# Second mixer: attention heads and state space written as steps beside the units, in a kept order, four units split ahead

## The chip, the cores and the metric

The kernel runs on one core of a Trainium2 chip. The metric is device time in microseconds (us) per execution, and a time is the median of several runs. The engines are TensorE (PE in the profile, with PEld for its weight loads), VectorE (DVE), ScalarE (ACT), GpSimd (POOL) and SyncE (SP), which issues the weight loads from memory.

## What is computed

A network on one sequence of 256 positions with 1024 channels, in float32: a first block of two layers and then a second block of two layers. The change touches only the mixer of the second block, which runs twice. Cut to it, the reference is:

```python
h = rms_norm_2(x, mix_norm[i])
proj = h @ w_in[i]
z, xbc, dt_raw, q, k, v = jnp.split(proj, splits, axis=-1)
xbc = jax.nn.silu(causal_depthwise_conv(xbc, conv_w[i], conv_b[i]))
y_ssd = ssd_mixer(xbc, dt_raw, z, dt_bias[i], a_log[i], d_skip[i], ssd_norm[i])
q = rms_norm_2(q.reshape(b, s, ATT_HEADS, ATT_HEAD_DIM), q_norm[i])   # 16 heads of 64
k = rms_norm_2(k.reshape(b, s, ATT_HEADS, ATT_HEAD_DIM), k_norm[i])
y_att = dilated_attention(q, k, v.reshape(b, s, ATT_HEADS, ATT_HEAD_DIM)).reshape(b, s, ATT_WIDTH)
x = x + jnp.concatenate([y_ssd, y_att], axis=-1) @ w_out[i]
```

`ssd_mixer` takes `dt = softplus(dt_raw + dt_bias)`, decays each of 16 heads by `exp` of a running sum of `dt * a` in two chunks of 128 positions, adds `x * d_skip`, gates by `silu(z)` and normalises in four groups. `dilated_attention` sums three strided windows, which the kernel does as one softmax with a mask and a table of multiplicities.

## The kernel before

The program has eleven stages in a row: ada0 and the even mixer, peer0, the odd mixer, peer1, and then ffn1_0, mix_0, ffn2_0, ffn1_1, mix_1, ffn2_1. mix_0 and mix_1 are two calls of `second_mixer` with their own weights, and only they and the order of their weights change.

Weights come as tiles of 1 MB, which SP loads (L154) into `w_raw`. One tile holds two *units* of 128x1024. Each float32 product is made of three products in a shorter format: a unit is copied by ACT into its high part `w_hi` (L171), and its low part `w_lo` is a subtraction (L162) on DVE or on POOL, as the letters of `E.pattern` say ("V" or "P", in turn). `w_hi` and `w_lo` have three buffers in the earlier stages; once L1590 has been passed, in ffn1_0, there are four of each and three of `w_raw`. A unit of a projection is then 24 matmuls of 128x256 (`mm3`, L199 to L201; L229 to L231 where the result has rows of positions).

A mixer uses 48 units for the input projection and 16 for the output. Its order in the text is: 16 units of q and k, each multiplied by the rms (L1384), squared (L338) and summed per head (L339); behind the second pair the parts of the normalised input `xn` (L1391) and the section that makes `dt` and its running sum `acum`; `rstd` of the sums; 8 units of v (`gemm_rows`); 8 blocks of two attention heads, each with two spreads of the norm (`spread2`, L357 and L358), scores (L1442 to L1445), softmax, transposes and the product with v (`attend`); 16 units of the convolution (first 8 `bc`, then 8 `xs`), each with one ACT and three DVE instructions (L1469, L1472) and a silu (L1460, L1461); the products of `bc` after its eighth, transposes of `xs` after each fourth; 8 units of `z` with a silu; then the state space, 8 blocks of two heads: a spread, three Relu (L1511), an Exp (L1513), two multiplications that give the decayed products `m` (L1515), two matmuls (L1518, L1519), the gate (L1521, L1522), a square (L1524) and its group sum (L1525); 8 units of the output projection for the attention's half (`accum` of blocks 8 to 15); `rstd` of the group sums; the normalised `y` in parts (L1537, L464, L465) and 8 units for the other half; and the residual (L423).

What runs when is not this order. A scheduler that knows only what depends on what and which buffers are free places the instructions of each engine, and puts heads, convolutions, state space and units between each other; only places in `in_order` keep the order of the text, and the second mixer has none.

Of the kernel before, what the change touches and what calls it, by code (L numbers as in the profile page):

```python
# [34 lines left out]
ADA = [b for c in range(8) for b in (8 + c, c)] + list(range(16, 96))  # L35

# [29 lines left out]
class Net:  # L66
# [108 lines left out]
    def units(self, ap):  # L175

        for k in range(ap.shape[0]):
# [4 lines left out]
    def prefetch(self, ap):  # L182

        u = self.units(ap)
# [244 lines left out]
    def attend(self, W, ps, mult, vrow, pv, o, between=None):  # L429
# [23 lines left out]
        pt = self.tp.tile([128, 512], F32, name="tp")  # L453
# [890 lines left out]
def second_mixer(E, i):  # L1344
# [3 lines left out]
    with ExitStack() as ctx:  # L1348
# [3 lines left out]
        yl = S.tile([128, 16, T], F32R, name="yl")  # L1352
        at = ctx.enter_context(tc.tile_pool(name="at", bufs=2, space=PSUM, side=E.side, reuse_waits="tile"))
        pvp = ctx.enter_context(tc.tile_pool(name="pv", bufs=1, space=PSUM, side=E.side, reuse_waits="tile"))
        E.tp = tp = ctx.enter_context(tc.tile_pool(name="tp", bufs=1, space=PSUM, side=E.side, reuse_waits="tile"))
# [4 lines left out]
        units = E.stage_units(io[f"mix_{i}_in"])  # L1360
# [6 lines left out]
        nc.gpsimd.dma_start(maskb, io["dilate_mask"])  # L1367
        identb = S.tile([128, 128], BF, name="identb")
        nc.vector.tensor_copy(identb, E.ident)
# [4 lines left out]
        for u in range(0, 16, 2):  # L1374
            pss = [mm.tile([128, T], F32, name="mm"),
                   pvp.tile([128, T], F32, name="pv") if u == 2 else mm.tile([128, T], F32, name="mm")]
            ws = [next(units) for _ in range(2)]
            if u == 0:
                E.gemms(pss, ws)
                rms = E.rms(tp.tile([128, T], F32, name="tp"))  # L1380
            for k in range(2):
                if u:
                    E.gemm(pss[k], ws[k])
                nc.vector.tensor_tensor(qk[:, u + k], pss[k], rms, op=OP.mult)  # L1384
                E.head_stat(W, stat[:, u // 8], qk[:, u + k], (u + k) % 8, 8, T, start=u + k == 0,
                            stop=(u + k) % 8 == 7)
            if u == 2:

                for c in range(NB):
                    t = E.nrm.tile([128, T], F32, name="sq", bufs=4)  # L1390
                    nc.vector.scalar_tensor_tensor(t, E.x[:, c], scale(c), rms, op0=OP.mult, op1=OP.mult)  # L1391
                    E.parts(xn[0][:, c], xn[1][:, c], t)

                dw = W.tile([128, 128], F32, name="dw", bufs=1)
                nc.scalar.dma_start(dw, io[f"mix_{i}_dt"])
                ps = at.tile([128, T], F32, name="at")
                E.gemm(ps[:16], E.split(dw, 128), 16, xn)
                dt, acum = (S.tile([16, T], F32, name=n) for n in ("dt", "acum"))
                e, t1, l, one = (t[:, k] for t in (S.tile([16, 2, T], F32, name=n) for n in ("r_hi", "r_lo"))
                                 for k in range(2))  # L1400
                db = E.s("dt_bias", i, p=16)
                nc.vector.memset(one, 1.0)
                nc.scalar.activation(t1, ps[:16], AF.Abs, bias=db)
                nc.scalar.activation(e, t1, AF.Exp, scale=-1.0)

                zero, ea = (S.tile([16, 1], F32, name=n) for n in ("zero", "ea"))
                nc.vector.tensor_scalar(zero, e[:, :1], 0.0, None, op0=OP.mult)
                nc.scalar.activation(ea, E.s("a_log", i, p=16), AF.Exp, bias=zero)
                nc.vector.tensor_scalar(dt, ps[:16], db, 0.0, op0=OP.add, op1=OP.max)
                log1p(E, l, e, t1)  # L1410
                nc.vector.tensor_tensor(dt, dt, l, op=OP.add)
                nc.vector.tensor_scalar(e, dt, ea, -1.0, op0=OP.mult, op1=OP.mult)
                for c in range(2):
                    sl = slice(c * 128, c * 128 + 128)
                    nc.vector.tensor_tensor_scan(acum[:, sl], one[:, sl], e[:, sl], 0.0, op0=OP.mult, op1=OP.add)
                rel = S.tile([16, 128], F32, name="rel")
                nc.vector.tensor_scalar(rel, acum[:, :128], acum[:, 127:128], None, op0=OP.subtract)
                ps = at.tile([128, 5, 16], F32, name="at")
                for k, src in enumerate((acum[:, :128], rel, acum[:, 128:], dt[:, :128], dt[:, 128:])):
# [335 lines left out]
```

## Time and profile before

| | us |
|---|---|
| median of 3 runs (3502.95 to 3520.05) | 3516.53 |
| the profiled execution | 3519.85 |
| its span in the profile | 3518.1 |
| mix_0, from 2308.9 to 2622.3 | 313.4 |
| mix_1, from 3006.9 to 3325.3 | 318.4 |

Over the whole span PE is busy for 97%, DVE for 67%, ACT for 53% and POOL for 27%. A mixer is read in three pieces that the trace marks well: the *start*, from the rms matmul (L323) to the first v matmul (L229); the *middle*, from there to the first Relu of the state space (L1511); and the *gated part*, from there to the residual (L423). In a row of the windows, the number behind an engine is its busy time and x its instructions; PEclk is the granted TensorE clock, 1.00 for 2.4 GHz and 0.50 for 1.2 GHz.

### The profile page before, as it was taken

What the parts mean: (1) busy time and instruction counts of PE and PEld (TensorE: products, weight loads), DVE (VectorE), ACT (ScalarE), POOL (GpSimd) and SP (SyncE); (2) the same over time, 40 slices, a digit from 0 to 9 for tenths busy, and PEclk for the clock granted to TensorE, in tenths of its full rate; (3) what the DMA queues carried; (4) which work ended last, traced back from release to release, by engine and by line L of the source; (5) the groups of instructions that cost most, each with busy time, mean ns of one, the idle gap of its engine ahead of it and who ended that gap; (6) DMA issues with size and microseconds to landing.
All of it is one profiled execution on the core that took longest, in us unless ns stands there. A gap on an engine that the chain in (4) does not pass through costs nothing.

```text
span 3518.1 us, 64405 instructions
## 1 busy us (share of the span) xinstructions
PE 3402.0 (97%) x26071; PEld 3169.4 (90%) x26071; DVE 2362.8 (67%) x4428; ACT 1881.7 (53%) x3561; POOL 937.1 (27%) x451
## 2 busy tenths in 40 slices
PE   5889999999999999999999999999999999999999
PEld 5679999999997579999999999977889999877899
DVE  5776878888885566878877776566654454665544
ACT  3444677644445445677644445446554444565443
POOL 0034000144443135000044444441142332302422
PEclk8989999999999899999999999999999999998899
DMA  6435444477774125444355555532335545423254
GB/s 251 179 114 185 167 150 148 144 263 269 271 261 153 37 73 180 168 145 147 142 191 186 186 191 193 180 137 97 120 110 189 182 180 182 148 94 110 98 190 144
DMA packets 85851, 576.64 MB, mean 164 GB/s; under 512 B 9855, under 2 KB 11248, under 8 KB 20016
## 3 DMA queue, kind: packets, MB, share of 16 engines
q1 hardware_dynamic: 82448, 567.35, 44.9%
q8 instruction: 204, 3.34, 0.4%
q0 software_dynamic: 1520, 3.30, 0.3%
q10 hardware_dynamic: 1584, 1.88, 0.2%
q14 instruction: 95, 0.78, 0.1%
HBM read 571.54 MB, written 1.34 MB: 163 GB/s over the span
## 4 chain that ended last, share of the span: by engine, by line
PE 85%; DVE 7%; ACT 3%; issue 1%; DMA 1%; POOL 0%; DVEq 0%; ACTq 0%; POOLq 0%
PE acc L200 15%; PE acc L201 14%; PE acc L199 14%; PE mm L199 9%; PE mm L201 9%; PE mm L200 9%; PE g L976 2%; PE g L978 2%; DVE w_lo L162 1%; ACT w_hi L171 1%; DMA w_raw<-peer_v 1%; PE at L357 1%; DVE wl L465 1%; PE stat L339 1%; PE pv L1518 1%
## 5 line engine op out<-in xcount | busy, mean ns | idle before, releaser
L171 ACT ACTIVATE w_hi<-w_raw 128x1024 fp32r<-128x1024 f32 x980 | 1037.4, 1059 | 1005.0 <-PE acc L200 416.3
L162 POOL TENSOR_TENSOR w_lo<-w_raw,w_hi 128x1024 fp32r<-128x1024 f32 x357 | 866.7, 2429 | 2351.5 <-ACT w_hi L171 1594.7
L162 DVE TENSOR_TENSOR w_lo<-w_raw,w_hi 128x1024 fp32r<-128x1024 f32 x623 | 765.7, 1229 | 339.1 <-ACT w_hi L171 322.3
L199 PE MATMUL mm<-xh,w_hi 128*128 128x256 f32 (+1 forms) x2568 | 734.9, 287 | 16.5 <-ACT xh L332 8.7
L200 PE MATMUL mm<-xl,w_hi 128*128 128x256 f32 (+1 forms) x2568 | 731.0, 285 | 3.1 <-DVE xl L333 1.6
L201 PE MATMUL mm<-xh,w_lo 128*128 128x256 f32 (+1 forms) x2568 | 730.5, 285 | 1.2 <-DVE w_lo L162 1.2
L200 PE MATMUL acc<-wl,w_hi 128*128 128x256 f32 x2048 | 574.5, 281 | 7.0 <-DVE wl L465 6.9
L199 PE MATMUL acc<-wh,w_hi 128*128 128x256 f32 x2048 | 573.8, 280 | 3.3 <-ACT wh L464 3.3
L201 PE MATMUL acc<-wh,w_lo 128*128 128x256 f32 x2048 | 573.6, 280 | 0.0
L199 PEld LDWEIGHTS mm<-xh,w_hi 128*128 128x128 f32 (+1 forms) x2568 | 488.7, 191 | 32.1 <-issue 18.5
L200 PEld LDWEIGHTS mm<-xl,w_hi 128*128 128x128 f32 (+1 forms) x2568 | 488.1, 190 | 11.1 <-DVE xl L286 4.2
L201 PEld LDWEIGHTS mm<-xh,w_lo 128*128 128x128 f32 (+1 forms) x2568 | 489.8, 191 | 5.0 <-DVE w_lo L162 2.4
L199 PE MATMUL acc<-xh,w_hi 128*128 128x256 f32 (+1 forms) x1536 | 449.1, 292 | 16.5 <-ACT xh L530 10.4
L200 PE MATMUL acc<-xl,w_hi 128*128 128x256 f32 (+1 forms) x1536 | 443.3, 289 | 15.6 <-DVE xl L532 15.1
L465 DVE TENSOR_TENSOR wl<-ring,wh 128x256 fp32r<-128x256 f32 x256 | 361.4, 1414 | 128.0 <-ACT wh L464 128.0
L201 PE MATMUL acc<-xh,w_lo 128*128 128x256 f32 (+1 forms) x1536 | 442.2, 288 | 0.1
L200 PEld LDWEIGHTS acc<-wl,w_hi 128*128 128x128 f32 x2048 | 385.5, 188 | 8.7 <-DVE wl L465 8.6
L199 PEld LDWEIGHTS acc<-wh,w_hi 128*128 128x128 f32 x2048 | 385.5, 188 | 3.7 <-ACT wh L464 3.7
L201 PEld LDWEIGHTS acc<-wh,w_lo 128*128 128x128 f32 x2048 | 385.5, 188 | 0.0
L199 PEld LDWEIGHTS acc<-xh,w_hi 128*128 128x128 f32 x1536 | 300.4, 196 | 18.9 <-ACT xh L530 11.3
L200 PEld LDWEIGHTS acc<-xl,w_hi 128*128 128x128 f32 x1536 | 298.3, 194 | 19.5 <-DVE xl L532 16.9
L201 PEld LDWEIGHTS acc<-xh,w_lo 128*128 128x128 f32 x1536 | 299.4, 195 | 1.7 <-issue 0.9
(452 smaller groups left out, 5961.7 us busy)
## 6 DMA issues: line engine op xcount, KB each, us to landing
w_raw<-ffn SPq DMA_DIRECT2D x132, 1024.0 KB, 4.8
w_raw<-peer_u SPq DMA_DIRECT2D x128, 1024.0 KB, 4.8
w_raw<-peer_v SPq DMA_DIRECT2D x128, 1024.0 KB, 4.8
w_raw<-mix_in SPq DMA_DIRECT2D x48, 1024.0 KB, 4.7
ring<-ada SPq DMA_DIRECT2D x56, 512.0 KB, 5.7
ada<-ada SPq DMA_DIRECT2D x20, 1024.0 KB, 4.8
w_raw<-mix_out SPq DMA_DIRECT2D x16, 1024.0 KB, 4.8
w_raw<-even_in SPq DMA_DIRECT2D x12, 1024.0 KB, 6.2
```

The costliest lines, as they stand in the source:

```text
L162: ins = e.tensor_tensor(out, a, hi, op=OP.subtract)
L171: self.nc.scalar.activation(hi[:, :n], src, AF.Copy)
L199: mm(ps, wh, xh, start=start, stop=False, skip_group_check=True)
L200: mm(ps, wh, xl, start=False, stop=False, skip_group_check=True)
L201: mm(ps, wl, xh, start=False, stop=stop, skip_group_check=True)
L339: self.nc.tensor.matmul(ps, self.esel[:, 30 - 2 * b:30 - 2 * b + 2 * nb], sq[:, :w], start=b == 0 if start is None else start, stop=b == n ...
L357: self.nc.tensor.matmul(ps, sel, hi, start=True, stop=False)
L465: return self.nc.vector.tensor_tensor(yl, src, yh.bitcast(F32), op=OP.subtract).ins
L976: nc.tensor.matmul(ps[:, t], oi[:, :, t], o1[:, :, t], start=t == 0, stop=False, skip_group_check=True)
L978: nc.tensor.matmul(ps[:, t], oi[:, :, t], o2[:, :, t], start=False, stop=t == TB - 1, skip_group_check=True)
L1518: mm_(pv[o:o + 64], xr[:, 0, hs], m[:, :256], start=True, stop=False, skip_group_check=True)
```

## The change

The units of the input projection come in another order (`MIX_IN`, of tiles of two units): two tiles of convolution, then one of z. The whole mixer keeps the order of its text on PE, DVE, ACT and SP (`in_order`). A `Flow` splits units up to four ahead, with pattern "V", so that every subtraction of the mixer is DVE's; 33 of 65 were POOL's in mix_0. The start multiplies four units before it squares any, makes the parts of `xn` one per unit, and leaves the `dt` section to `steps()`, whose pieces follow the units of the convolution one by one. Attention is made of ticks: tick t makes the scores of head t-1, the transposes of head t-2, the two spreads of block t/2 if t is even, and the product with v of head t-3. A unit of v in the second half and a unit of z has one tick before it, a unit of convolution 0.4. Transposes take the banks `tp` and `st` in turn. The second half of a silu (`pending`) waits for the next tick or unit, products and transposes of `xs` (`later`) for one unit each. In the gated part a block is: the gate of the block before, one output unit (blocks 0 to 5), the group sums, the decay of the next two heads, and the two matmuls of each of its own heads. Units 14 and 15 of the output follow the last block, with `rstd` between them, and `finish` of block b+2 stands behind unit b.

Cut to its core, the diff is (removed lines stand in the functions above):

```diff
+MIX_IN = list(range(12)) + [12, 13, 20, 14, 15, 21, 16, 17, 22, 18, 19, 23]
...
-        units = E.stage_units(io[f"mix_{i}_in"])
+        flow = Flow(E, chain(E.stage_units(io[f"mix_{i}_in"]), E.units(io[f"mix_{i}_out"])), 2)
+        order.enter_context(E.in_order(*(e.engine for e in (nc.tensor, nc.vector, nc.scalar, nc.sync))))
...
+        first = [bank(), bank(), bank(), pvp.tile([128, T], F32, name="pv")]
+        flow.split()
+        E.gemms(first[:2], [next(flow), next(flow)])
+        flow.split(3)
+        E.gemm(first[2], next(flow))
+        rms = E.rms(tp.tile([128, T], F32, name="tp"))
+        flow.split()
+        E.gemm(first[3], next(flow))
+        flow.split()
+        for u in range(4):
+            scaled(u, first[u])
+        for u in range(4):
+            squared(u)
+        nc.vector.tensor_copy(identb, E.ident)
+        for u in range(4, 16):
+            ps = bank()
+            E.gemm(ps, next(flow))
+            stats()
+            scaled(u, ps)
...
+            flow.split()
+            squared(u)
+            if c < NB:
+                E.parts(xn[0][:, c], xn[1][:, c], t)
...
+        def steps():
...
+            E.gemm(ps[:16], dws, 16, xn)
...
+            nc.scalar.activation(l, t1, AF.Ln)
+            yield
...
+        def tick(t):
+            def between():
+                if t > 1:
+                    next(heads[t - 2], None)
+                while pending:
+                    pending.pop()()
+                if t < 16 and t % 2 == 0:
+                    spread(t // 2)
+            if 1 <= t < 17:
+                head(t - 1, between)
+            else:
+                between() if t < 18 else None
+            if t >= 3:
+                next(heads[t - 3], None)
+                if (t - 3) % 2:
+                    blk = (t - 3) // 2
+                    E.parts(yh[:, 8 + blk], yl[:, 8 + blk], pvs[-1])
...
+        for p in MIX_IN[12:]:
+            for u in (2 * p - 24, 2 * p - 23):
+                attention(1 if u >= 16 else 0.4)
+                ps = bank()
+                E.gemm(ps, next(flow), x=xn)
+                if later:
+                    later.popleft()()
...
+                next(pieces, None)
+        attention(19)
...
+        def out(k):
+            E.accum(acc, next(flow), yh[:, k], yl[:, k], k == 8, k == 7)
+            flow.split()
+
+        decay(0)
+        decay(1)
         for blk in range(8):
+            while pending:
+                pending.pop()()
+            if blk < 6:
+                out(8 + blk)
+            gated()
+            if blk < 7:
+                decay(2 * blk + 2)
+                decay(2 * blk + 3)
+            states(blk)
+        pending.pop()()
+        out(14)
+        gated()
+        r = E.rows(S, "s", E.rstd(E.nrm, stat[:4, 0], [4, T], 256), lambda t: t[:4, 0], [16, 2, T])
+        out(15)
...
+        finish(0)
+        finish(1)
+        for blk in range(8):
+            out(blk)
+            if blk < 6:
+                finish(blk + 2)
```

What it does to the rows of an engine is shown at three places of mix_0. Lines above 36 move down by 4 and those of the mixer by more, so L162 is L166 after, and L1384 is L1391. The first place is the start, on DVE; `rs_v` is the rms, `dw` the weights of `dt`, and `tp`, `mm` and `pv` are banks of accumulators. Before:

```order
L162 TENSOR_TENSOR w_lo<-dw,w_hi 128x128
L252 TENSOR_SCALAR rs_v_27247<-tp 128x256
L253 SCALAR_TENSOR_TENSOR rs_v_27247<-rs_v_27247,rs_r_27248 128x256
L254 TENSOR_TENSOR rs_v_27247<-rs_v_27247,rs_r_27248 128x256
L255 SCALAR_TENSOR_TENSOR rs_v_27247<-rs_v_27247,rs_r_27248 128x256
L1384 TENSOR_TENSOR qk<-mm,rs_v_27247 128x256 x3
L162 TENSOR_TENSOR w_lo<-w_raw,w_hi 128x1024
L1384 TENSOR_TENSOR qk<-pv,rs_v_27247 128x256
```

And after:

```order
L166 TENSOR_TENSOR w_lo<-w_raw,w_hi 128x1024 x3
L256 TENSOR_SCALAR rs_v_27299<-tp 128x256
L257 SCALAR_TENSOR_TENSOR rs_v_27299<-rs_v_27299,rs_r_27300 128x256
L258 TENSOR_TENSOR rs_v_27299<-rs_v_27299,rs_r_27300 128x256
L259 SCALAR_TENSOR_TENSOR rs_v_27299<-rs_v_27299,rs_r_27300 128x256
L166 TENSOR_TENSOR w_lo<-w_raw,w_hi 128x1024 x2
L1391 TENSOR_TENSOR qk<-mm,rs_v_27299 128x256 x3
L1391 TENSOR_TENSOR qk<-pv,rs_v_27299 128x256
```

The subtraction of `dw` has left the place ahead of the rms, and two subtractions of units stand between the rms and the first multiplication by it.

The second place is one pair of attention heads in the middle, on PE. Before, the scheduler's order (r_hi and r_lo are the spreads' operands, identb and maskb the mask of the scores, pts the transposed weights of a head):

```order
L455 MATMUL tp<-cst,p 128x128
L199 MATMUL mm<-yh,w_hi 128x256
L455 MATMUL tp<-cst,p 128x128 x2
L200 MATMUL mm<-yl,w_hi 128x256
L201 MATMUL mm<-yh,w_lo 128x256
L199 MATMUL mm<-yh,w_hi 128x256
L357 MATMUL at<-r_hi,bsel 128x256
L358 MATMUL at<-r_lo,bsel 128x256
L200 MATMUL mm<-yl,w_hi 128x256
L460 MATMUL pv<-pts,v 64x256
L461 MATMUL pv<-pts,v 64x128
L201 MATMUL mm<-yh,w_lo 128x256
```

After, one tick between two units:

```order
L1504 MATMUL at<-maskb,identb 128x384
L1505 MATMUL at<-qk 128x128
L1507 MATMUL at<-qk 128x256
L459 MATMUL stat<-cst,p 128x128 x3
L361 MATMUL at<-r_hi,bsel 128x256
L362 MATMUL at<-r_lo,bsel 128x256
L361 MATMUL at<-r_hi,bsel 128x256
L362 MATMUL at<-r_lo,bsel 128x256
L464 MATMUL pv<-pts,v 64x256
L465 MATMUL pv<-pts,v 64x128
L203 MATMUL mm<-yh,w_hi 128x256
```

The matmuls of the heads, which stood singly among those of a unit, stand in one piece between two units.

The third place is the gated part, on ACT: decay of the heads (Relu, Exp), the gate's square, and the copies of the units. Before:

```order
L1511 ACTIVATE m<-at,col 128x128 x4
L1513 ACTIVATE m<-m 128x384
L1511 ACTIVATE m<-at,col 128x128
L1524 ACTIVATE sq<-v 128x256
L1511 ACTIVATE m<-at,col 128x128
L171 ACTIVATE w_hi<-w_raw 128x1024
L1513 ACTIVATE m<-m 128x384
```

After, blocks 5 to 7 (p and pts are the decayed products of an even and of an odd head):

```order
L1659 ACTIVATE sq<-z 128x256
L175 ACTIVATE w_hi<-w_raw 128x1024
L1639 ACTIVATE p<-at,col 128x128 x3
L1641 ACTIVATE p<-p 128x384
L1639 ACTIVATE pts<-at,col 128x128 x3
L1641 ACTIVATE pts<-pts 128x384
L1659 ACTIVATE sq<-z 128x256
L1639 ACTIVATE p<-at,col 128x128 x3
L1641 ACTIVATE p<-p 128x384
L1639 ACTIVATE pts<-at,col 128x128 x3
L1641 ACTIVATE pts<-pts 128x384
L1659 ACTIVATE sq<-z 128x256 x2
```

Every block has the same five pieces in the same order, and in blocks 6 and 7 no unit's copy stands among them.

## Rows read from the trace of the kernel before

**Rows 1.** Stretches: window, length, busy (x) of PE PEld DVE ACT POOL, PEclk, DMA, GB/s

```profile
2200.00:2240.00 40.00, 40.00 (x338) 40.00 (x337) 21.84 (x26) 18.35 (x25) 16.79 (x7) 1.00 0.53 185
2312.90:2379.10 66.20, 58.74 (x393) 47.41 (x392) 37.03 (x58) 28.01 (x46) 22.99 (x10) 0.92 0.36 129
3010.80:3066.80 56.00, 53.99 (x393) 44.74 (x392) 32.78 (x61) 28.05 (x46) 13.02 (x7) 1.00 0.43 152
2379.10:2529.20 150.10, 148.53 (x937) 120.97 (x935) 96.81 (x241) 90.21 (x178) 24.89 (x12) 1.00 0.31 111
3066.80:3216.90 150.10, 149.04 (x940) 121.38 (x938) 98.19 (x242) 90.25 (x178) 21.88 (x11) 1.00 0.31 111
2529.20:2616.60 87.40, 84.69 (x484) 64.62 (x485) 37.22 (x73) 44.11 (x99) 33.27 (x14) 0.88 0.25 89
3216.90:3319.60 102.70, 98.79 (x482) 72.09 (x482) 37.19 (x73) 44.22 (x99) 33.15 (x14) 0.73 0.21 75
3231.90:3272.90 41.00, 41.00 (x122) 23.27 (x121) 10.55 (x29) 15.88 (x42) 4.69 (x2) 0.50 0.07 26
2545.00:2585.00 40.00, 40.00 (x228) 26.80 (x228) 18.53 (x43) 24.45 (x59) 11.87 (x5) 1.00 0.15 54
```

**Rows 2.** Timeline, start of mix_0: start, length, engine, line, [idle before <-releaser]

```profile
2312.95 5.15 DVE L162 TENSOR_TENSOR w_lo<-dw,w_hi 128x128 fp32r<-128x128 f32 x1 [0.21 <-PE mm L200]
2320.84 2.74 PE L339 MATMUL stat<-sq,cst 128*16 128x256 f32 x6 [3.60 <-ACT sq L338]
```

**Rows 3.** Timeline of PE in the even mixer: one head's matmuls between two units

```profile
126.31 0.34 PE L626 MATMUL at<-maskb,identb 128*128 128x384 bf16 x1
128.70 0.38 PE L357 MATMUL at<-r_hi,bsel 8*128 8x256 f32 x1
129.37 0.39 PE L199 MATMUL mm<-xh,w_hi 128*128 128x256 f32 x1
```

**Rows 4.** Groups by line, middle of mix_0: count | busy us, mean ns | idle before

```profile
L171 ACT ACTIVATE w_hi<-w_raw 128x1024 fp32r<-128x1024 f32 x33 | 34.9, 1058 | 31.8 <-PE mm L200 21.9 <-PE mm L231 6.8 <-issue 3.0
L162 POOL TENSOR_TENSOR w_lo<-w_raw,w_hi 128x1024 fp32r<-128x1024 f32 x12 | 29.4, 2452 | 130.1 <-ACT w_hi L171 130.1
L162 DVE TENSOR_TENSOR w_lo<-w_raw,w_hi 128x1024 fp32r<-128x1024 f32 x22 | 26.9, 1222 | 18.1 <-ACT w_hi L171 18.0
L1469 ACT ACTIVATE cv<-mm,sm 128x256 f32<-128x256 f32 x16 | 8.9, 556 | 0.1
L1472 DVE SCALAR_TENSOR_TENSOR cv<-mm,sm,cv 128x254 f32<-128x254 f32 x16 | 7.7, 481 | 0.5
L437 DVE TENSOR_REDUCE nm<-at 128x1 f32<-128x128 f32 x16 | 4.7, 291 | 8.2 <-PE at L1445 7.9
L1490 PE MATMUL tp<-cst,xs 128*128 128x128 f32 x16 | 3.6, 297 | 1.0 <-DVE xs L1461 1.0
L1478 PE MATMUL tp<-bc 128*128 128x256 f32 x8 | 2.7, 424 | 0.0
L1479 PE MATMUL tp<-bc 128*128 128x128 f32 x8 | 1.5, 274 | 0.0
```

**Rows 5.** Timeline of ACT in the middle of mix_0: Exp of one head's scores

```profile
2417.26 0.72 ACT L442 ACTIVATE p<-at,nm 128x128 f32<-128x128 f32 x2
```

**Rows 6.** Timeline, gated part of mix_0: one block's pieces on ACT, DVE and PE

```profile
2554.10 0.88 ACT L1511 ACTIVATE m<-at,col 128x128 f32<-128x128 f32 x3 [0.75 <-PE pv L1519]
2555.64 0.51 ACT L1513 ACTIVATE m<-m 128x384 f32<-128x384 f32 x1
...
2557.68 0.59 PE L1525 MATMUL tp<-sq,cst 128*4 128x256 f32 x2
2557.80 0.75 DVE L1515 SCALAR_TENSOR_TENSOR m<-m,col,cbm 128x256 f32<-128x256 f32 x2 [0.87 <-ACT m L1513]
...
2558.21 0.65 PE L1518 MATMUL pv<-m,bc 128*64 128x256 f32 x2
...
2559.00 0.38 PE L357 MATMUL at<-acum_hi,identr 16*128 16x256 f32 x1
```

More of the change, by code (lines that the diff above doesn't have):

```diff
@@ L173, in split, with units @@
         return hi, lo
-    def units(self, ap):
-        for k in range(ap.shape[0]):
+    def units(self, ap, order=None):
+        for k in order or range(ap.shape[0]):
             t = self.load(ap[k])
@@ L1367, in second_mixer @@
         nc.gpsimd.dma_start(maskb, io["dilate_mask"])
+        dw = W.tile([128, 128], F32, name="dw", bufs=1)
+        nc.scalar.dma_start(dw, io[f"mix_{i}_dt"])
         identb = S.tile([128, 128], BF, name="identb")
-        nc.vector.tensor_copy(identb, E.ident)
         v = S.tile([128, 2, D], F32, name="v")
         xn = yh[:, :NB], yl[:, :NB]
-        stat = st.tile([16, 2, T], F32, name="stat")
[L1374 to L1380, printed above, removed]
-            for k in range(2):
[L1382 to L1419, printed above, removed]
-                    nc.tensor.transpose(ps[:, k], src, E.ident[:16, :16])
-                col = S.tile([128, 5, 16], F32, name="col")
-                nc.vector.tensor_copy(col, ps)
-                acum = E.rows(S, "acum", acum)
@@ new lines, in second_mixer, with turned, spread @@
+        heads, pvs, turns = {}, [], [0]
+        def turned():
+            turns[0] += 1
+            return (tp, st)[turns[0] % 2].tile([128, 512], F32, name=("tp", "stat")[turns[0] % 2])
+        def spread(blk):
+            ps = at.tile([128, 2, T], F32, name="at")
+            for k in range(2):
+                E.spread2(ps[:, k], r, k, blk)
+            for k in range(2):
+                u = 8 * k + blk
+                nc.vector.scalar_tensor_tensor(qk[:, u], qk[:, u], E.s("k_norm2" if k else "q_norm2", i), ps[:, k],
+                                               op0=OP.mult, op1=OP.mult)
@@ new lines, in sums, with head @@
+        def sums(h):
+            if h % 2 == 0:
+                pvs.append(pvp.tile([128, T], F32, name="pv"))
+            return pvs[-1]
+        def head(h, between):
+            blk, o = h // 2, h % 2 * 64
+            ps = at.tile([128, 384], F32, name="at")
+            mm_(ps, identb, maskb, start=True, stop=False, skip_group_check=True)
+            mm_(ps[:, 0:128], qk[o:o + 64, blk, 0:128], qk[o:o + 64, 8 + blk, 0:128], start=False, stop=False,
+                skip_group_check=True)
+            mm_(ps[:, 128:384], qk[o:o + 64, blk, 128:256], qk[o:o + 64, 8 + blk], start=False, stop=True,
+                skip_group_check=True)
+            heads[h] = E.attend(W, ps, mult, [v[:, tt, h * 64:h * 64 + 64] for tt in range(2)], lambda: sums(h), o,
+                                between, turned)
+            next(heads[h])
@@ new lines, in second_mixer, with decay @@
+        attention(19)
+        while later:
+            later.popleft()()
+        for _ in pieces:
+            pass
+        ctx2.close()
+        acc = E.accs(ctx.enter_context(tc.tile_pool(name="acc", bufs=1, space=PSUM, side=E.other(), reuse_waits="tile")))
+        stat = tp.tile([16, 2, T], F32, name="tp")
+        ms = {}
+        def decay(h):
+            ps = at.tile([128, T], F32, name="at")
+            E.spread(ps, E.identr[:, h:h + 1].to_broadcast([16, 128]), *acums)
+            m = ms[h] = W.tile([128, 384], F32, name=("p", "pts")[h % 2])
+            for k, sl in enumerate((slice(0, 128), slice(128, 256), slice(128, 256))):
+                nc.scalar.activation(m[:, k * 128:k * 128 + 128], ps[:, sl], AF.Relu, bias=col[:, k, h:h + 1],
+                                     scale=-1.0)
+            nc.scalar.activation(m, m, AF.Exp, scale=-1.0)
+            for k, sl in enumerate((slice(0, 256), slice(256, 384))):
+                nc.vector.scalar_tensor_tensor(m[:, sl], m[:, sl], col[:, 3 + k, h:h + 1], cbm[:, h // 4, sl],
@@ L1526, in second_mixer @@
-        E.pattern = "P"
-        units = E.units(io[f"mix_{i}_out"])
-        for k in range(8, 16):
-            E.accum(acc, next(units), yh[:, k], yl[:, k], k == 8, False)
-        r = E.rows(S, "r", E.rstd(E.nrm, stat[:4, 0], [4, T], 256), lambda t: t[:4, 0], [16, 2, T])
-        for blk in range(8):
+                m, hs = ms.pop(h), slice(h * 64, h * 64 + 64)
+                mm_(pv[o:o + 64], xr[0][:, 0, hs], m[:, :256], start=True, stop=False, skip_group_check=True)
+                mm_(pv[o:o + 64, 128:], xr[0][:, 1, hs], m[:, 256:], start=False, stop=True, skip_group_check=True)
@@ L1541, in second_mixer @@
+        order.close()
         E.pattern = "VVP"
```

256 lines of the change are left out of this document (157 added, 99 removed).

## Prediction

> **What bounds the kernel now.** I read the stretches first [rows 1]. A stretch of matmuls of 128x256 with nothing between them holds 338 in 40.00 us, 0.1183 us each, so a unit of 24 is 2.84 us. That is the price that a unit cannot go under at the 2.4 GHz clock. Then I cut each mixer into start, middle and gated part [rows 1]. Start: 66.2 and 56.0 us. Middle: 150.1 in both. Gated part: 87.4 and 102.7. Together 303.7 and 308.8; the rest of the program has the same instructions before and after, and I take it as unchanged. In the middle PE is busy for 148.53 of 150.10, DVE for 96.81 and ACT for 90.21: PE is the bound there. In the gated part PE is again nearly always busy, but at a clock of 0.88 and 0.73. So what can be won is of three kinds: idle time of PE at the start, time that PE is busy with something shorter than it looks (changes of the tile's shape, waits inside a run of matmuls), and time at the low clock.
>
> The two starts tell the first kind. They hold the same matmuls (x393), and the first is 10.2 longer. Its PE is idle for 66.20 - 58.74 = 7.5 against 2.0, and at a clock of 0.92 it loses 0.08 x 66.2 = 5.3. The cause of the idle time is one subtraction of the dt weights that took 5.15 on DVE ahead of the rms; the squares came late and PE sat for 3.60 [rows 2]. The second mixer does not show it.
>
> **The start.** From the rms matmul to v the new order has 14 units, 14 x 2.84 = 39.8, and no dt section (its 24 matmuls, 2.8, move to the middle). The 16 sums of squares cost what is left in the second mixer's start: 56.0 - 39.8 - 2.8 = 13.4, or 0.83 each with all changes of shape. The lower bound is half of what three took at the low clock, 2.74 / 3 / 2 = 0.46 [rows 2]. Their place behind a unit stays the same, so I take 0.75, near the upper end: 15 of them 11.2, and 0.6 for the rms matmul. One wait is new. Unit 4 needs a bank that only a multiplication by the rms frees, and by the order of DVE two subtractions stand ahead of it; one of them waits for its copy on ACT: 1.06 + 1.22 = 2.3 [rows 4]. Behind that multiplication are queued all of DVE's later subtractions, but four units are split by then. Start: 39.8 + 11.2 + 0.6 + 2.3 = **54**, from 51.6 (no wait) to 57. That is -12 in mix_0 and -2 in mix_1.
>
> **The middle.** It has 8 + 16 + 8 = 32 units, 32 x 2.84 = 90.9; 150.1 - 90.9 = 59.2 is for 16 heads and the small products. In the even mixer, which already has a kept order, a head's matmuls stand in one piece and take 129.37 - 126.31 = 3.06 with four spread matmuls, 0.67 of it for these [rows 3], so 2.39 without. Eight ticks have spreads: 8 x 3.06 + 8 x 2.39 = 43.6. Products and transposes are 3.6 + 2.7 + 1.5 = 7.8 [rows 4]. So 59.2 - 43.6 - 7.8 = 7.8 is what changes of shape and short waits cost before, and goes: **-8**. Added are the dt matmuls, 2.8, the last sum of squares, 0.75, and the transposes of dt's columns, put at 0.6 by the group of four in [rows 4] (4 x 0.297 at most 1.2): **+4.2**.
>
> The kept order also makes waits that the scheduler filled. Twelve subtractions come from POOL to DVE, 12 x 1.22 = 14.7, and dt's instructions, about 7 by an estimate from the start (DVE is busy for 37 there against some 30 without them); DVE has then 96.8 + 14.7 + 7 = 118.5 to do in 150, ACT its 90 and two table loads. Both engines fit. But each head has a wait of DVE for scores (7.9 / 16 = 0.5 before [rows 4]) and for an Exp, 0.72 [rows 5], and each unit of the convolution waits for ACT's 0.556. Behind a DVE that waits stand the next subtraction and, four units later, PE. I take 5.2 for all of this: 1.1 for rstd's rows in the v units, 1.5 for the `at` bank that dt's pieces hold, and 2.6 for DVE falling behind by some 0.9 in each of three groups of six units. The lower end is 0, the upper 13, which is the third rival's sum below with four more. Middle: 150.1 - 8 + 4.2 + 5.2 = **151.5**, +1.4 in each mixer, from 146 to 160.
>
> **The gated part.** A block's pieces on PE are a unit, 2.84; the group sum, 2558.21 - 2557.68 = 0.53; the spreads of two heads, the same four matmuls as in a tick, 0.7; the two matmuls of two heads, 2 x (2559.00 - 2558.21) = 1.58 [rows 6]; and a change of shape, 0.2. Six blocks with a unit: 6 x 5.85 = 35.1, with the first spreads 35.8, less one group sum that the first block lacks: 35.3. The chain that has to be ready is Relu, Exp, Relu, Exp and a multiplication, 2 x (0.88 + 0.51) + 0.75 = 3.5 [rows 6]. In a block with a unit 5.8 cover it. In block 6 only 1.58 + 0.53 + 0.7 = 2.8 does, and ACT has a copy and a square ahead of it: a wait of 0.7 to 3.5, I take 2.7. Block 7 has less beside it, 1.4 to 3.5, I take 3.0. With their own work, 2.8 and 2.1, these two are 10.6. Then units 14 and 15 with a group sum, 6.2, and three waits for the last gate, rstd and the first finished block, which I put at 3.2 (from 0, as unit 15 is 2.84 of cover, to 7, twice the chain above). Last 8 units and three spreads with changes, 22.7 + 1.5 = 24.2. Sum: 35.3 + 10.6 + 6.2 + 3.2 + 24.2 = 79.5, about 80.
>
> The clock is the unknown. At 0.50, 41 us held 122 matmuls, where 40 us at 1.00 held 228 [rows 1], so a microsecond at the low clock loses about 0.48. mix_0's gated part lost 0.12 x 87.4 = 10.5 of full speed to it and mix_1's 0.27 x 102.7 = 27.7 [rows 1]. In the new order PE waits for some 9 us, within blocks 6 and 7 and behind them, and I take one low stretch of about 10 us there, half of what mix_0 lost: **+5**. Gated part: **85**, -2.4 in mix_0 and -17.7 in mix_1. The lower end is 80, the upper mix_1's 103.
>
> **The sum** is -12.2 - 2.0 + 1.4 + 1.4 - 2.4 - 17.7 = -31.5. Against the profiled execution's 3519.85, of which the span is 3518.1, this is 3488. The median of the runs shown lies 3.3 lower than that execution, so the runs after may lie as much below. What leaves POOL, 33 subtractions per mixer, costs nothing beside this: POOL is free, and nobody else waits for it.
>
> **Rivals.** First: PE alone decides and all waits are hidden, at the full clock. Start 51.6, middle 150.1 - 8 + 4.2 = 146.3, gated part 79.5: 277.4 per mixer, 2 x 277.4 against 612.5, -57.7, or **3462**. For it speaks that PE is the bound in every part. Against it speaks that in the kept order any late copy stops all that stands behind it.
>
> Second: the clock stays low for most of the gated part, in both mixers, as in mix_1 now: 102.7 each. Then +15.3 and 0 in place of -2.4 and -17.7, the sum is about +4, **3524**, no change. For it speaks that mix_1 runs at 0.50 for 41.00 us although its PE is busy for all of them, and that the same instructions at 1.00 in mix_0 show no cause in this part [rows 1]. Against it, the kept order puts a unit between the pieces from the first block on.
>
> The Trainium skill bears on this (TensorE: Matmul & The Clock Gate, section "Loop structure matters more than you think"): it says that the loop nest decides whether matmuls run at full clock, and that those which follow each other without waits do. The row of 41 us speaks against it as the only rule, since PE was busy all along. By the rule alone blocks 0 to 5 run at full clock, and only blocks 6 and 7 are in danger; that is the forecast.
>
> Third, on the other side: DVE and ACT wait for each other and pace the middle. If no wait is covered, DVE loses 16 x (0.5 + 0.72) + 16 x 0.556 = 28.4, and has 118.5 + 28.4 = 147. The v units with four heads hold about 24 of it (8 x 1.22 for subtractions, and a head at 2.3 + 1.2, from what is left of 96.8 without subtractions, 16 x 3 x 0.48 of convolutions and 24 silus). The other 24 units then have 123 for DVE, against 151.5 - 34 = 117.5 for PE (8 x 2.84 + four ticks): about 6, with the silus' own waits for ACT 9, so 160. PE then stops in each group of six units and loses its clock, one 41-us stretch per mixer as in [rows 1], 18 to 20 each. The sum is -31.5 + 2 x 9 + 2 x 18 = +22, **3540**. It decides once DVE's waits in a group of six units exceed about 4: PE has there six units, 3.6 ticks and a share of the products, 28, and DVE by the same parts about 24. For it speaks that a kept order lets no later subtraction pass a waiting one; against it, silus, norms and subtractions stand between the reductions and what needs their Exp.
>
> That the order is not kept can be left out: the rows of the changed kernel's order are the text's.
>
> **How the numbers follow.** About 0.5% is what a measurement here can tell from no change, 3499 to 3534. The forecast has 0.55, of which 0.11 lies above 3499; the first rival 0.18, the second 0.14, the third 0.13. So faster 0.44 + 0.18 = 0.62, same 0.11 + 0.14 = 0.25, slower 0.13. The forecast's own bounds are wide, -57 to beyond +20 if all ends fell together, which they won't. For 8 in 10 the range leaves out the third rival and the quickest part of the first: 3452 to 3527.
>
> **What would show it.** Right: the first multiplications of the start follow rms without a 5-us subtraction, start 52 to 57 in both mixers; a tick takes 2.4 to 3.1 on PE; the middle stays within 146 to 155; the gated part has one low stretch around blocks 6 and 7 and none of 41 us. Wrong: PE rows in the middle with idle time behind a subtraction of DVE (third rival), or PEclk near 0.7 over the gated part (second). If both starts are 52 and no stretch is low, the first was right.

## The result and the profile after

The changed kernel takes 3529.86 us (median of 12 runs) against 3504.18 of the kernel before in the same series: a ratio of 1.0072, 95% interval 1.0056 to 1.0088. It is slower by 0.7%, where 3488 was forecast, with a range of 3452 to 3527.

Cut at the same places as [rows 1], the changed mixers look like this (windows: length, busy and count of PE, PEld, DVE, ACT, POOL, PEclk, DMA, GB/s; the two starts, the two middles, the two gated parts):

```profile
2313.45:2363.96 50.51, 47.80 (x348) 40.11 (x346) 30.37 (x51) 21.86 (x38) 0.00 (x0) 1.00 0.44 163
3022.90:3076.07 53.17, 50.45 (x348) 42.48 (x346) 30.37 (x51) 21.89 (x38) 0.00 (x0) 0.94 0.43 156
2363.96:2537.52 173.56, 161.16 (x964) 131.77 (x963) 110.87 (x269) 92.76 (x183) 0.00 (x0) 0.91 0.27 98
3076.07:3244.10 168.03, 156.19 (x970) 128.86 (x969) 110.93 (x269) 92.43 (x184) 0.00 (x0) 0.95 0.29 101
2537.52:2625.96 88.44, 72.67 (x484) 60.56 (x485) 44.74 (x86) 45.23 (x99) 2.40 (x1) 0.86 0.24 85
3244.10:3329.37 85.27, 69.17 (x478) 57.17 (x479) 44.72 (x85) 45.22 (x99) 2.40 (x1) 0.90 0.24 87
```

The start is shorter by one unit here, since the third unit now stands ahead of the rms matmul; with its 2.84 us it is 53.3 and 56.0. The middles are 23.5 and 18 us longer than the 150.1 of [rows 1]. PE is idle there for 173.56 - 161.16 = 12.4 and 11.8, and the lower clock takes, by estimate, 0.09 x 173.6 = 15.6 and 0.05 x 168.0 = 8.4. What is left, 145.6 and 147.8, is the 146.3 of the first rival.

A second profile of the kernel before (its execution took 3504.63) changes the picture of what the change was measured against. Gated part of the second mixer, and a stretch of 41 us in it:

```profile
3221.57:3304.35 82.78, 78.72 (x482) 60.66 (x482) 37.19 (x72) 43.97 (x99) 33.16 (x14) 0.96 0.27 94
3236.60:3277.60 41.00, 40.21 (x235) 27.61 (x235) 18.03 (x42) 24.63 (x57) 14.70 (x7) 1.00 0.22 73
```

The 41 us at 0.50 of [rows 1] are not there; the part takes 82.8, not 102.7. All other pieces agree with the first profile within 0.3 us. So the profiled execution of before, 3519.85, had an accident of some 20 us that the other one, 3504.63, lacks. That most executions lack it is argued from their times (seven of the twelve lie between 3499 and 3505, five between 3513 and 3524) and not shown by profiles.

Where TensorE stops in the changed middle, the timeline of mix_0 shows. The names: `at` is a bank of accumulators, shared by heads and dt's pieces; L1451 reads dt's matmuls, L1470 is the running sum, L1475 transposes it, L1477 copies the columns, L1458 is the Ln.

```profile
2416.36 1.52 DVE L1612 SCALAR_TENSOR_TENSOR cv<-mm,sm,cv 128x255 f32<-128x255 f32 x3 [2.44 <-ACT cv L1608]
2418.93 0.47 DVE L1451 TENSOR_SCALAR dt<-at,sm 16x256 f32<-16x256 f32 x1
2419.45 0.38 PE L361 MATMUL at<-r_hi,bsel 16*128 16x256 f32 x1 [2.22 <-DVE dt L1451]
...
2431.51 1.28 ACT L1458 ACT_TABLE_LOAD   x1
2433.24 1.28 ACT L446 ACT_TABLE_LOAD   x1
2436.42 0.84 PE L459 MATMUL stat<-cst,p 128*128 128x128 f32 x3 [1.66 <-ACT p L455]
...
2453.09 1.22 DVE L166 TENSOR_TENSOR w_lo<-w_raw,w_hi 128x1024 fp32r<-128x1024 f32 x1
2454.22 0.72 DVE L1470 TENSOR_TENSOR_SCAN acum<-s_lo,s_hi 16x128 f32<-16x128 f32 x2
2454.68 0.23 PE L1475 MATMUL at<-cst,acum 16*128 16x16 f32 x1 [2.85 <-DVE acum L1470]
...
2464.78 0.35 PE L361 MATMUL at<-r_hi,bsel 16*128 16x256 f32 x1 [1.80 <-DVE col L1477]
```

Four times PE asks for something that is queued on DVE or ACT behind a convolution, a subtraction or two table loads, and no unit may pass: 2.22 + 1.66 + 2.85 + 1.80 = 8.5 us. The second mixer has the same four. The granted clock falls behind such waits: it is 0.61 over the 16 us behind the one of 2.85, which hold the one of 1.80, and 1.00 in a later stretch without any. The first two rows show these, and the next two the gated part (blocks 6 and 7, blocks 2 and 3):

```profile
2456.00:2472.00 16.00, 14.20 (x63) 12.29 (x63) 8.44 (x22) 4.53 (x10) 0.00 (x0) 0.61 0.18 66
2480.00:2496.00 16.00, 16.00 (x118) 14.28 (x118) 11.09 (x29) 8.73 (x23) 0.00 (x0) 1.00 0.18 67
2578.00:2590.00 12.00, 7.94 (x32) 4.54 (x33) 3.71 (x10) 3.95 (x11) 0.00 (x0) 0.50 0.10 43
2548.00:2560.00 12.00, 10.12 (x77) 8.02 (x76) 7.14 (x15) 8.14 (x20) 0.00 (x0) 1.00 0.25 89
```

In the gated part PE's timeline shows the first output unit waiting for the last `z` (L1577), and the group sums waiting for the gate's square. The sums shown are those of blocks 4, 5 and 6; the first of them is like the four before it, and the other two stand in blocks 6 and 7:

```profile
2539.00 0.38 PE L203 MATMUL acc<-yh,w_hi 128*128 128x256 f32 x1 [2.56 <-DVE z L1577]
...
2573.07 0.59 PE L1667 MATMUL tp<-sq,cst 128*4 128x256 f32 x2 [0.84 <-ACT sq L1659]
2579.03 1.02 PE L1667 MATMUL tp<-sq,cst 128*4 128x256 f32 x2 [3.90 <-ACT sq L1659]
2585.71 1.02 PE L1667 MATMUL tp<-sq,cst 128*4 128x256 f32 x2 [3.02 <-ACT sq L1659]
```

### The profile page after: what moved, and what is told of

Its sections match the earlier page's. It is cut to its first block, busy times and chain, and to the rows that moved or that the text cites. A ratio compares the mean times of both kernels' runs of the same rounds, so it can differ in the third digit from the quotient of the medians.

```text
span 3528.2 us, 64240 instructions
## 1 busy us (share of the span) xinstructions
PE 3368.0 (95%) x26071; PEld 3163.5 (90%) x26071; DVE 2401.2 (68%) x4488; ACT 1880.4 (53%) x3559; POOL 791.9 (22%) x391
## 4 chain that ended last, share of the span: by engine, by line
PE 81%; DVE 9%; ACT 5%; issue 1%; DMA 1%; POOL 0%; ACTq 0%; DVEq 0%; POOLq 0%
PE acc L204 14%; PE acc L203 14%; PE acc L205 14%; PE mm L203 9%; PE mm L204 9%; PE mm L205 9%; DVE w_lo L166 2%; PE g L980 2%; PE g L982 2%; ACT w_hi L175 1%; DMA w_raw<-peer_v 1%; DVE wl L469 1%; DVE xl L290 1%; PE pv L1325 1%; PE mm L233 1%
## 5 line engine op out<-in xcount | busy, mean ns | idle before, releaser
L166 POOL TENSOR_TENSOR w_lo<-w_raw,w_hi 128x1024 fp32r<-128x1024 f32 x298 | 722.8, 2427 | 2505.6 <-ACT w_hi L175 1775.1
L166 DVE TENSOR_TENSOR w_lo<-w_raw,w_hi 128x1024 fp32r<-128x1024 f32 x682 | 839.2, 1231 | 384.7 <-ACT w_hi L175 368.6
```

What stands on the lines that cost most here:

```text
L166: ins = e.tensor_tensor(out, a, hi, op=OP.subtract)
```

## The experiments

The lengths below are from one profiled execution each; "mixers" is the sum of both, from the end of the residual before to the start of their own: before 601.0 (second profile; 621.2 in the first), after 633.0. Two cautions on small differences. The median of before was 3504 to 3511 by series, so kernels are better compared by the ratios than by the medians. And the profiled execution was up to 5 us from its kernel's median, but in e3 and e7 8 and 9 above it, in e9, e10 and e12 14, 15 and 11 below. The v units of mix_0, whose text is the same in after and e4, took 40.2 us at a clock of 0.87 in one and 35.6 at 1.00 in the other.

| kernel | median | ratio to before (95%) | mixers |
|---|---|---|---|
| after | 3529.86 | 1.0072 (1.0056 to 1.0088) | 633.0 |
| e1, dt pieces from unit 12 | 3516.38 | 1.0027 (1.0004 to 1.0051) | 611.7 |
| e3, dt pieces with slack | 3510.25 | 1.0009 (0.9983 to 1.0034) | 608.0 |
| e4, group sums last | 3526.97 | 1.0059 (1.0033 to 1.0085) | 618.7 |
| e6, 9 subtractions on GpSimd | 3533.49 | 1.0064 (1.0042 to 1.0087) | 632.4 |
| e7, dt wholly in the start | 3506.04 | 1.0005 (0.9991 to 1.0020) | 604.2 |
| e8, e7 with halves of units | 3496.41 | 0.9980 (0.9960 to 1.0001) | 587.2 |
| e5, order free | 3456.36 | 0.9881 (0.9838 to 0.9923) | 554.8 |
| e9, order kept on PE alone | 3505.37 | 0.9979 (0.9949 to 1.0010) | 591.7 |
| e10, kept on DVE and ACT | 3513.81 | 1.0009 (0.9992 to 1.0025) | 605.1 |
| e11, e8 with order free | 3455.22 | 0.9837 (0.9795 to 0.9880) | 553.0 |
| e12, e5 with GpSimd in the gated part | 3470.33 | 0.9884 (0.9840 to 0.9928) | 555.4 |

**The second profile of before.**

> The kernel before once more, for a second profile of it. The first one had 41 us at half clock in the gated part of the second mixer, and its execution was 3519.85 where most take 3500 to 3507. If that stretch is an accident of that execution, this one's gated part is 86 to 92 in both mixers and the forecast's -17.7 was counted from a time that most executions do not have; if it belongs to the kernel, it is about 102 again.

Shown above: 82.8. The first mixer's gated part was 87.3 and 87.4, the second's 102.7 and 82.8, below even the 86 to 92 that were expected if the stretch was an accident.

**dt pieces behind units 12 to 15 and the units of v.**

```diff
+            if u == 11:
+                E.parts(*dws, dw)
+                pieces = steps()
+            elif u > 11:
+                next(pieces)
...
                 flow.split()
+                next(pieces, None)
                 if half == 0 and u == 0:
...
-                next(pieces, None)
         attention(19)
```

> The changed kernel with the dt section back in the start: its pieces run behind units 12 to 15 of q and k and then behind the units of v, not behind the units of the convolution. All else stays. Theory A (TensorE waits in the middle because it reads results of the dt pieces too soon behind a DVE that is a unit late, and then also loses its clock): the three waits of 2.6, 3.2 and 2.1 us leave each middle, some of the low clock with them, so the middle falls from 173.6 and 168.0 to 150 to 162 and the time from about 3530 to 3500 to 3516. Theory B (all subtractions on DVE overload it, and DVE and ACT wait for each other): the same waits appear at other places, the middle stays above 164, the time within 4 of 3530. Theory C (the heads in one piece and the kept order cost it as such): as B.

v units and the rest of the first middle, and a spread in v:

```profile
2380.18:2425.70 45.52, 38.70 (x152) 26.80 (x151) 26.35 (x62) 21.55 (x37) 0.00 (x0) 0.89 0.27 93
2425.70:2537.78 112.08, 110.58 (x790) 94.94 (x788) 83.17 (x203) 69.92 (x144) 0.00 (x0) 1.00 0.33 114
```

```profile
2393.84 0.38 PE L361 MATMUL at<-r_hi,bsel 16*128 16x256 f32 x1 [4.22 <-DVE r_hi L355]
```

Without dt the convolution and z take 112.1 where they took 133.4, at the full clock and with PE busy for all but 1.5. That is against theory B and C for this stretch: the same kept order, the same heads in one piece and the same subtractions run without a wait. The v units lose 5 to 10 instead, as dt's pieces there delay the norm's rows, so the whole is 13 us and not 14 to 30. The middles, 157.6 both, lie within the 150 to 162 of theory A.

**The pieces in the middle, with slack.**

```diff
             E.gemm(ps[:16], dws, 16, xn)
             nc.vector.memset(one, 1.0)
-            yield
...
+            yield
             ps = at.tile([128, 5, 16], F32, name="at")
...
                 nc.tensor.transpose(ps[:, k], src, E.ident[:16, :16])
-            yield
```

> The changed kernel with the dt section still in the middle, but its first reads of the accumulator stand right behind its matmuls, one more unit passes before the transposes of the running sum, and the copy of the columns stands right behind them. No work is added or taken. Theory A: the waits of 2.6 (spread behind dt's read), 3.2 (transposes behind the sums) and about 2 (spread behind the copy) shrink to under 1 each, the time falls to 3505 to 3522; the two table loads around Ln stay, with their wait of about 2. Theory B and C: 3526 to 3534.

Convolution and z of mix_0, and the one long wait that is left there:

```profile
2414.50:2536.34 121.84, 116.36 (x819) 99.31 (x817) 89.19 (x219) 74.38 (x152) 0.00 (x0) 0.97 0.30 104
```

```profile
2445.25 1.09 PE L459 MATMUL stat<-cst,p 128*128 128x128 f32 x3 [3.85 <-ACT p L455]
```

Three lines moved by a unit, with no work taken, give 20 us. The three waits for dt's results are gone; the one behind Ln's table loads has grown from 1.7 to 3.9; here a reciprocal of dt's, 1.74 us on DVE, also stands ahead of that head's reduction.

**Group sums last in a block.**

```diff
-            gated()
             if blk < 7:
                 decay(2 * blk + 2)
                 decay(2 * blk + 3)
             states(blk)
+            gated()
```

> The changed kernel with one move in the gated part: the group sums of a block stand behind the next block's decay and state matmuls, not ahead of them. The middle is unchanged. If TensorE's waits of 0.8 in blocks 1 to 5 and of about 4 in blocks 6 and 7 are that it asks for the gate's square too soon, the gated part falls by 4 to 10 in each mixer, the time to 3510 to 3522. If the chain of Relu, Exp and multiplications sets the pace there, the waits move to the state matmuls and the time stays within 4 of 3530.

```profile
2541.17:2625.75 84.58, 73.27 (x484) 60.81 (x485) 44.73 (x86) 44.55 (x99) 2.40 (x1) 0.86 0.25 89
3242.37:3322.90 80.53, 68.96 (x478) 56.53 (x479) 44.73 (x86) 44.55 (x99) 2.40 (x1) 0.92 0.26 92
```

```profile
2585.41 0.66 PE L1651 MATMUL pv<-p,bc 128*64 128x256 f32 x1 [2.33 <-DVE y L1656]
```

4 to 5 us per mixer, about the five waits of some 0.84; in blocks 6 and 7 the waits moved to the state matmuls. These wait there for the gate before them to read their one accumulator (y), and that read is queued on DVE behind the multiplications of the next heads, so there the chain sets the pace, through DVE's order. The time moved by 3, which the interval does not tell from nothing.

**Subtractions back on GpSimd.**

```diff
-                    flow.split()
+                    flow.split(1, "P" if u % 3 == 2 else "V")
...
-                    flow.split()
+                    flow.split(1, "P" if u % 2 else "V")
```

> The changed kernel with 9 of 24 subtractions of each mixer's convolution and z units back on GpSimd, every third of the first and every second of the second; the order of everything else stays. Theory B: DVE has 11 us less to do in a stretch of 130, the middle falls by 8 or more per mixer, the time to 3514 or less. Theory A and C: DVE's load is not what TensorE waits for, 3524 to 3536.

```profile
2407.58:2543.89 136.31, 124.67 (x819) 106.46 (x817) 89.03 (x210) 74.66 (x152) 19.37 (x9) 0.91 0.27 93
```

136.3 against 133.4, and 3533.49: DVE's load is not it, and that half of theory B falls. Whether the order in which DVE and ACT wait for each other costs is not tested here, but below (e10).

**dt wholly in the start, and halves of output units.** The first makes two parts of xn per unit (c from 2u - 8) and runs a piece behind each of units 8 to 15; the second adds:

```diff
-            if blk < 6:
+            if blk < 4:
                 out(8 + blk)
-            gated()
+            else:
+                half(10 + blk // 2)
...
             states(blk)
+            gated()
```

> The changed kernel with the whole dt section in the start: the parts of xn are made two per unit, so that they are ready behind unit 7 of q and k, and the pieces of dt run behind units 8 to 15, the last one behind the rstd of the norm. Theory A (where the dt pieces stand is what costs the middle): v units 33 to 37, convolution and z 109 to 114 at a clock near 1.00, start 58 to 63, each mixer 20 shorter than changed, time 3484 to 3498. Theory B (DVE and ACT pace the middle) or C (the kept order as such): convolution and z stay above 120, time above 3515.

> The kernel of the run before (dt in the start) with the gated part spread: group sums behind the state matmuls, and in blocks 4 to 7 half an output unit each in place of whole units in 4 and 5 and none in 6 and 7. If the waits of 4.3 and 3.7 in blocks 6 and 7 and the low clock of some 10 us behind them come from the missing unit, the gated part falls from 85 to 88 to 74 to 80 and the time by another 12 to 22 to 3466 to 3484. If the chain of Relu, Exp and multiplications needs more than half a unit beside it, waits of 1 to 2 us per block come instead, and the time falls by 6 or less.

v units, then convolution and z, of the first; the gated parts of the second:

```profile
2382.24:2421.04 38.80, 35.01 (x147) 24.52 (x146) 22.11 (x52) 18.52 (x32) 0.00 (x0) 0.96 0.31 109
2421.04:2533.13 112.09, 110.59 (x790) 94.93 (x788) 83.17 (x203) 70.49 (x147) 0.00 (x0) 1.00 0.32 114
```

```profile
2530.64:2611.67 81.03, 72.50 (x484) 61.15 (x485) 44.62 (x85) 44.32 (x99) 2.40 (x1) 0.89 0.26 92
3213.11:3293.54 80.43, 69.42 (x478) 58.15 (x479) 44.56 (x86) 44.32 (x99) 2.40 (x1) 0.94 0.27 92
```

The convolution came as expected. The time is 8 us above the upper end of what was expected of e7: v units kept 38.8 and 41.8 (PE waits there for the norm's rows, 2.3, and for the first head's Exp, about 1), and the start, counted here from the residual before it as the expectation does, took 62.1 and 63.3 (57.5 and 60.2 in the changed kernel). The halves gave 5 to 7 per mixer in the gated part and 10 us of the time, between the 12 to 22 and the 6 or less that were expected. The part stayed above 74 to 80: PE's waits for the first output unit (2.6 and 1.7) and behind block 7 (2.9) stay, and the state matmuls now wait five times, 3.5 and 5.6 us in all, as the second reading had it.

**The order not kept, kept on PE alone, kept on DVE and ACT alone.** One line is left out, or has fewer engines:

```diff
-        order.enter_context(E.in_order(*(e.engine for e in (nc.tensor, nc.vector, nc.scalar, nc.sync))))
```

> The changed kernel, same text, but its order in the second mixer is not kept: the scheduler places the instructions as in the kernel before. Theory A (a late read of dt's pieces stops what stands behind it): the scheduler lets units pass the waiting matmuls, the waits of 2 to 3 us in the middle shrink, the time is 3500 to 3520. Theory C (heads in one piece and the kept order cost as such): 3495 or less. If the kept order helped on the whole and only lost at dt: 3530 or more.

> The changed kernel with its order kept on TensorE alone; VectorE, ScalarE and SyncE are the scheduler's. If TensorE's own order is what costs (a matmul that asks for a late result holds all units behind it), the time stays at 3515 to 3530. If it is the order of DVE and ACT (a waiting instruction there makes the results late), TensorE's order does no harm by itself: 3456 to 3480.

> The changed kernel with its order kept on VectorE and ScalarE, TensorE and SyncE being the scheduler's. By the first reading (TensorE's order costs): 3456 to 3480, since units pass the matmuls that wait. By the second (DVE's and ACT's order makes the results late): 3500 to 3530, since what TensorE could take in place of the waiting one comes late too.

Middles and gated parts with a free order, and the transposes of the running sum in it:

```profile
2367.43:2515.15 147.72, 146.89 (x964) 120.83 (x963) 108.34 (x267) 91.71 (x182) 0.00 (x0) 1.00 0.32 115
3036.37:3184.08 147.71, 147.44 (x969) 121.40 (x969) 108.37 (x266) 91.72 (x182) 0.00 (x0) 1.00 0.33 115
2515.15:2590.55 75.40, 70.24 (x484) 59.63 (x485) 42.27 (x86) 44.33 (x99) 2.39 (x1) 0.93 0.29 99
3184.08:3256.91 72.83, 68.15 (x482) 57.48 (x481) 42.26 (x85) 44.35 (x99) 2.40 (x1) 0.95 0.29 102
```

```profile
2437.55 0.25 DVE L1468 TENSOR_SCALAR rel<-acum 16x128 f32<-16x128 f32 x1
...
2440.26 0.23 PE L1472 MATMUL at<-cst,acum 16*128 16x16 f32 x1
```

With the same text, the same units and the same subtractions, 73 us go (by the ratios 67, by the mixers 78). The transposes stand 2.5 us behind what they read, and PE is idle for 0.8 and 0.3 of a middle. This is more than theory A gave (3500 to 3520) and within theory C (3495 or less): what the kept order costs is not the dt section alone. Middle and gated part of mix_0 with PE's order kept (v; convolution and z; gated), and then with DVE's and ACT's:

```profile
2365.35:2403.82 38.47, 35.03 (x147) 24.50 (x147) 21.48 (x50) 18.13 (x32) 0.00 (x0) 0.96 0.31 110
2403.82:2528.76 124.94, 116.59 (x819) 99.22 (x817) 87.04 (x216) 75.33 (x151) 0.00 (x0) 0.99 0.29 102
2528.76:2604.92 76.16, 67.80 (x484) 57.31 (x485) 42.75 (x85) 44.65 (x99) 2.39 (x1) 0.93 0.28 98
```

```profile
2359.98:2393.32 33.34, 33.34 (x145) 22.75 (x145) 20.53 (x46) 16.72 (x30) 0.00 (x0) 1.00 0.35 127
2393.32:2521.46 128.14, 119.86 (x821) 101.78 (x819) 90.19 (x225) 74.72 (x155) 0.00 (x0) 0.96 0.28 99
2521.46:2605.12 83.66, 73.39 (x484) 60.41 (x485) 46.83 (x85) 44.56 (x99) 2.39 (x1) 0.88 0.26 90
```

Neither reading was right alone: e9, 3505.37, lies between its two ranges, and e10, 3513.81, within that of the second reading. Against the free order's 554.8 the mixers have 37 more with PE's order and 50 more with that of DVE and ACT, and 78 with all. PE's order costs in v (5 per mixer) and in the convolution (10); DVE's and ACT's in the convolution (13) and in the gated part (8 to 11). With PE's order alone the waits for dt's results are gone from the convolution, and PE waits there for `xs` (3.3) and for heads' weights (4.2); with that of DVE and ACT it waits for DVE to free a bank (5.0). As these two profiles come from executions 14 and 15 below their medians, the 37 and 50 are rather low; SyncE's order was not tested by itself.

**Free order with the other text, and with GpSimd.**

> The kernel with dt in the start and halves of output units, its order not kept. If the scheduler evens out what the text puts where, it is the free order's 3456 within 6. If the halves also serve the scheduler in blocks 6 and 7, the gated part falls from 75 and 73 to 68 to 72 and the time to 3444 to 3450.

> The changed kernel with a free order, and the subtractions of the output units (those split in the gated part) on GpSimd, as before the change. If the gated part's 75 and 73, against 87 and 83 in the kernel before, come from GpSimd no longer subtracting beside DVE, it goes back to 80 to 87 and the time to 3470 to 3485. If they come from the new text (heads two by two ahead, four buffers of decayed products, y in time), it stays below 77 and the time within 5 of 3456.

```profile
2371.89:2405.25 33.36, 33.36 (x148) 23.18 (x147) 21.63 (x51) 18.89 (x33) 0.00 (x0) 1.00 0.37 126
2405.25:2517.01 111.76, 110.93 (x790) 95.05 (x788) 81.25 (x201) 69.99 (x145) 0.00 (x0) 1.00 0.32 114
2517.01:2590.86 73.85, 69.82 (x484) 58.41 (x485) 42.08 (x86) 43.92 (x99) 2.39 (x1) 0.95 0.29 101
```

```profile
2516.79:2590.54 73.75, 69.57 (x484) 58.90 (x485) 38.38 (x73) 43.74 (x99) 30.98 (x13) 0.93 0.29 102
3183.93:3259.05 75.12, 68.17 (x482) 57.41 (x481) 39.84 (x74) 43.76 (x99) 31.03 (x13) 0.95 0.28 99
```

The first three rows are the v units, convolution and z, and gated part of e11, the last two the gated parts of e12. The free order evens the texts out: 3455 and 3456. As e8 and e11 have one text, kept and free, they also show what the kept order costs once dt is out of the middle: 587.2 against 553.0, 34 in place of 78. Convolution and z have almost nothing of it (112.1 against 111.8); v has 5 to 8 per mixer, the gated part 7 to 9, the start 2.

The gated part keeps its 73.8 and 75.1 with GpSimd subtracting again, so what it gained against 87 and 83 is the new text's and not GpSimd's leaving. The time expected of e12 was missed: the median of its four runs is 14 above e5's, but its mixers, from the fastest of the four, are not, and why is open. By the ratios e5 and e11 beat the kernel before by 1.2 and 1.6%.

## Why the prediction was wrong

**The step that failed** is the middle's third term, the waits that a kept order makes: 5.2 was taken per mixer, with an upper end of 13. It was 27.3 and 21.7 (173.6 and 168.0 less 146.3). Two things were missed. I looked for waits of DVE and ACT for each other and summed busy times, 118.5 in 150; but PE does not wait for a sum, it waits for one result. Each dt piece was put on DVE behind the convolution and subtraction of its unit, and what PE reads of it stood one unit later or none: 8.5 us, where I had 1.5 for the `at` bank and nothing for the transposes, the columns and Ln's loads. (It takes the order of both sides: with PE's alone kept, in e9, these waits are gone.) The other is the clock, 15.6 and 8.4 in the middle, which I counted only in the third rival. (5.2 of the 15.6 is in the v units, 0.13 x 40.15, and not every execution has it: e4 had 1.00 there.) That rival's sign was right, by its second half (PE stops and loses its clock). Of its first half, DVE's load is refuted: subtractions taken from DVE brought nothing, and dt taken out of the stretch brought the clock back to 1.00. But that the kept order of DVE and ACT makes results late stands: alone it costs 13 us in convolution and z (e10).

By the Trainium skill (PSUM — Partial Sum Buffer, section "Engine vs sequencer instructions") matmuls start and complete in program order and the queues of ScalarE and VectorE are strict first-in-first-out. The trace agrees: the matmuls of a ready unit stood 2.85 us behind a transpose of 0.23. So a kept order is a promise that every result is there when its reader is at the head; the scheduler before had kept it, and e5 kept it again.

**The sum's base.** -17.7 of the -31.5 was mix_1's gated part, 102.7 to 85. The second profile has 82.8. Against the second profile that term is +2.2, and the whole forecast would have been some 12 below 3504. I saw that the execution was 3.3 above the median of three runs, and did not ask whether its 41 us at half clock were part of every run.

**What held.** Start: 54 forecast, 53.3 and 56.0 measured, and the 5.15-us subtraction is out of the way. Work of PE in the middle: 146.3 forecast without waits, 147.7 with a free order, so the 8 us for changes of shape were there. In blocks 6 and 7 the waits were 3.9 and 3.0 (2.7 and 3.0 taken), with one stretch of 12 us at 0.50.

**What came out by luck.** Gated part: 85 forecast, 88.4 and 85.3 measured, but not by the terms of the sum. PE was idle there for 15.8 and 16.1, where the sum had 8.9: five waits of some 0.84 and the 2.56 of the first output unit were not in it. The clock took up to 0.14 x 88.4 = 12.4 and 0.10 x 85.3 = 8.5, where it had 5. What is left for the work is some 60 to 65 by estimate (65 with a free order: 70.24 of busy time less 0.07 x 75.4), where the sum had 79.5 - 8.9 = 70.6. Too much work and too few waits offset each other. Summed with these lengths, the forecast misses by 38.6 in the middles, 3.7 in the gated parts and 1.3 in the starts, 43.6: 3531.6 against 3529.9.

**The first rival**, all waits hidden, was 3462 and had 0.18. The text of the change comes to about that time with the order left free (3456), and does hide the waits of the middle (147.7 for 146.3). The gated parts are 75.4 and 72.8 for its 79.5, though with PE idle for some 5 and clocks of 0.93 and 0.95; there its work was put too high as well.

Open is what share of the free order's gain over before comes from which edit. GpSimd's leaving the gated part is excluded. Of the start's 15 in mix_0 (70.3 to 55.6, from the residual before) only 3 is the dt section's leaving, since e11 has that section in the start and takes 58.7. The rest was not taken apart.

## What to carry to other kernels

An order kept by hand is costed by its readers: for each matmul that reads another engine's result, list what stands ahead of that result in that engine's queue, and give it a unit more than that. Write the steps well and let the scheduler place them first; keep an order only where it beats that, and per engine. Before a term is taken from a slow stretch of one profile, look at a second profile of the same kernel.

## What was not expected of the hardware

The granted clock of the same program in the same place was 0.73 over 102.7 us in one execution and 0.96 over 82.8 in another, with the same instructions ahead of it. Around PE's waits of 3.9 and 3.0 us in blocks 6 and 7 it was 0.50 over 12 us, behind the one of 2.85 us 0.61 over 16, and with dt's pieces gone from convolution and z it stayed at 1.00 (e1, e7). The Trainium skill's rule that the loop nest decides (TensorE: Matmul & The Clock Gate, section "Loop structure matters more than you think") agrees with the second and not with the first.
